# VectorE in place of GpSimd for the whole-tile sums, other first banks in the second FFN layer and its row work issued tile by tile

## The chip, the core and the metric

The kernel runs on one core of one Trainium2 chip. A core has TensorE (PE in the profile; its weight loads are PEld), VectorE (DVE), ScalarE (ACT), GpSimd (POOL) and SyncE (SP), which here only issues DMAs. Each engine works through its own queue in order. The metric is the device time in microseconds.

## The reference

One trunk layer is applied to two groups of rows with the same parameters: 1024 latent rows (the sample) and 128 prompt rows, 1152 rows of width 1024. First comes a mixing sub-layer of four gated branches, which this change does not touch until its last product, the output projection. Then an FFN of hidden width 2816, and a final norm:

```
x  = x + g1 * (merged @ w_o)                 # output projection
h2 = rmsnorm(x, norm2_g) * (1 + sc2) + sh2
a, b = split(h2 @ ffn_w1)                    # 1024 -> 2 x 2816
x  = x + g2 * ((silu(a) * b) @ ffn_w2)       # 2816 -> 1024
y  = rmsnorm(x, final_norm_g)
```

Everything is float32.

## The kernel before

Every float32 operand of a matmul is split in two parts of a rounded format: a high part (ScalarE casts it) and the rest (VectorE subtracts the high part from the source). A product of two operands is then three matmuls into the same bank (mm3, lines 257 to 259; lines 1372 to 1374 in the first FFN layer). So each tile that TensorE reads costs one ScalarE and one VectorE instruction, whatever else it needs.

Both FFN layers use a two-by-two block scheme with seven block products in place of eight (products 0 to 6). It needs sums and differences of blocks of the weights (S1 to S4), of the activations (T1 to T4) and of the results. A sum of 128x512 elements is called a whole-tile sum here.

The stages that matter:

*Output projection* (lines 1450 to 1477). Three column groups c of 384 rows each, two halves hf of 512 columns. For each, TensorE multiplies into three banks; VectorE multiplies them by the gate g1 into xt (line 1472), the sum with x is made by GpSimd for c = 0 and 1 and by VectorE for c = 2 (line 1473), ScalarE sums squares (line 1474), and the new x goes to DRAM (x1_d, line 1476). norm_to_quarters (line 1283) then normalises a group, transposes it on TensorE in four steps kp and makes the sums of its quarters: two on VectorE (lines 1300, 1301), two on GpSimd (1302, 1303), all of 128x192, and splits them (1306, 1307).

*First FFN layer*. Twenty-two pairs j of a gate tile and a value tile, seven products each. w_prepare(j, i) (line 1327) makes the weight tile of product i, three products ahead (LEAD = 3): it loads the raw weights at i = 0, sums blocks with GpSimd at i = 1, 4 and 5 (w_sum, line 1322), casts (1340) and subtracts (1341). A pair uses four PSUM tiles f0, f1, f3 and f4 of two banks each; Pair.evac (line 1377) reads them out after each product, f1 after product 1, f0 after product 2, f3 after product 5 and f4 after product 6 (line 1396). Pair.store (line 1399) writes the pair's result to DRAM and, for every second pair, forms four whole-tile row sums with GpSimd (line 1414).

*Second FFN layer*. Seven products n of 11 steps jj each. A step multiplies four row tiles q, 12 matmuls; in products 0, 4 and 5 a fifth bank, pp, takes three more matmuls for the prompt rows (ask_part, "ask" in the names), whose share of product 6 stands at the end. prepare(n, jj) (line 1549) is called three steps ahead: it takes the next tile from the generator weights(jj) (line 1526), which loads blocks into br (16 buffers) and forms differences with GpSimd (lines 1532, 1536, 1540), loads the row tile ar (4 buffers), and splits both (parts, lines 1522 and 1523) into ah and bh (4 buffers each), or for some tiles into slot, a pool of 10 buffers (line 1258). A pool J of eight banks is opened before the first product (line 1579). After the eleven steps evacuate(n, q) (line 1642) reads out each bank. From product 4 on it also does the row work in the same place: residual (times g2, plus x1), squares, first_half (times the final norm's weight) and finish (norm, output). Of these the sums on lines 1611, 1627 and 1651 and the product on line 1622 are GpSimd's. The power of -1/2 in every norm is GpSimd's as well (line 280).

What sets the order: the program is traced in the order of the Python code, and a scheduler then places each engine's instructions by a simulated time, earlier code first where several are ready; a block under high priority or ahead(n) moves up. Buffers are given out in that same pass. So the code's order is a preference, and the order on an engine is fixed when the kernel is built.

Of the kernel before, what the change touches and what calls it, by code (L numbers as in the profile page):

```python
# [15 lines left out]
P = 128  # L16
# [68 lines left out]
def kernel(ctx: ExitStack, tc: tile.TileContext, A: dict, O: dict):  # L85
# [1197 lines left out]
    def norm_to_quarters(xn3, c):  # L1283

        cs = c * CH
        for kp in range(4):
# [15 lines left out]
            G.tensor_sub(u[1][:, 0], b22, b12)  # L1302
            G.tensor_sub(u[1][:, 1], b21, u[0][:, 1])
# [23 lines left out]
    def w_prepare(j, i):  # L1327
# [3 lines left out]
        if i == 1:  # L1331
            w_sum(j, "S1", "A21", "A22", G.tensor_add)
            w_sum(j, "S2", "S1", "A11", G.tensor_sub)
        if i == 4:
            w_sum(j, "S3", "A11", "A21", G.tensor_sub)
        if i == 5:
            w_sum(j, "S4", "A12", "S2", G.tensor_sub)
# [12 lines left out]
    class Pair:  # L1350
# [48 lines left out]
        def store(self):  # L1399
# [12 lines left out]
            for o, t, x, y, op in (("S1", s1, a21, a22, G.tensor_add), ("S2", s2, s1, a11, G.tensor_sub),  # L1412
                                   ("S3", s3, a11, a21, G.tensor_sub), ("S4", s4, a12, s2, G.tensor_sub)):
                op(t, x, y)
                put(o, t)
# [32 lines left out]
    for c in range(NCH):  # L1448
        sts = [small("wst", [P, 4], bufs=4) for _ in range(3)]
        for hf in range(2):  # L1450
# [18 lines left out]
            for q in range(3):  # L1469
# [3 lines left out]
                (V if c == NCH - 1 else G).tensor_add(x, x, t)  # L1473
# [52 lines left out]
    def weights(jj):  # L1526
# [3 lines left out]
        for kh, nh in ((0, 1), (1, 1)):  # L1530
            x = w2_load(kh, nh, jj)
            G.tensor_sub(x, x, b)
# [3 lines left out]
        G.tensor_sub(x, b21, b)  # L1536
# [3 lines left out]
        G.tensor_sub(x, b22, b12)  # L1540
# [8 lines left out]
    def prepare(n, jj):  # L1549
# [5 lines left out]
        bt = zt("bh", [P, 2, 512], 4, F32R) if n < 6 or jj < 4 else slot("bh", [P, 2, 512], F32R)  # L1555
# [3 lines left out]
        elif n in PROMPT:  # L1559
            plain[n, jj] = ready[n, jj][1]  # L1560

# [17 lines left out]
    open_psum("J", "left", m=8)  # L1579
# [5 lines left out]
    for h in range(2):  # L1585
        hs = slice(h * KH, h * KH + KH)
        dma(askr[:, hs], ask_d[h])
# [16 lines left out]
    def residual(i, h, c):  # L1604
# [6 lines left out]
        G.tensor_add(c, c, x1)  # L1611
# [6 lines left out]
    def first_half(i, c):  # L1618
# [3 lines left out]
        G.tensor_mul(c, c, fng[:, :512])  # L1622

    def last_product(i, c, ps):
        t = half_slot("lp")
        V.tensor_mul(t, ps, g2rows[i == 8][:, 512:])
        G.tensor_add(c, c, t)
# [14 lines left out]
    def evacuate(n, q, ps):  # L1642
# [6 lines left out]
        elif n == 2:  # L1649
            V.tensor_add(a["c21"], a["c11"], ps)  # L1650
            G.tensor_add(a["c12"], a["c12"], a["c21"])
        elif n == 3:
            V.tensor_add(a["c21"], a["c21"], ps)
        elif n == 4:
            V.tensor_add(a["c11"], a["c11"], ps)
            first_half(q, a["c11"])
        elif n == 5:
            V.tensor_add(a["c21"], a["c21"], ps)
            V.tensor_add(a["c22"], a["c12"], ps)
            residual(q, 1, a["c12"])  # L1660
            first_half(4 + q, a["c21"])
            residual(4 + q, 1, a["c22"])
            finish(4 + q, a["c21"], a["c22"])
# [4 lines left out]
    def ask_part(n, pp, jj):  # L1668
        kh, nh = PROMPT[n]
        k = kh * KH + jj  # L1670
        mm3(pp, (askt[:, 0, k], askt[:, 1, k]), plain.pop((n, jj)), jj == 0, jj == KH - 1)
# [15 lines left out]

    def product(n, qs):
        ps = {q: bank("f2", "m") for q in qs}
        pp = bank("fp", "m") if n in PROMPT and n < 6 else None  # L1690
        for jj in range(KH):
# [7 lines left out]
            if pp is not None:  # L1699
                ask_part(n, pp, jj)  # L1700
# [5 lines left out]
    for n in range(7):  # L1706
# [9 lines left out]
        product(n, range(4))  # L1716
    pp = bank("fp", "m")
# [160 lines left out]
```

## Time and profile before

| what | value |
|---|---|
| median of 3 timed runs | 2130.51 us (2131.29, 2124.45, 2130.51) |
| the profiled execution's own time | 2123.89 us |
| its span, first to last instruction | 2122.1 us |
| mean granted clock of TensorE | 0.987 |
| GpSimd busy, instructions | 575.8 us, 516 |

The stages in the span: projection to about 1303 us, then the norm of the last group and the first pair to 1378, the first FFN layer to 1848, the second to 2108, and a tail without matmuls. In the views, a row of a group names its line, engine and operation, then output<-inputs, the shapes, the count, busy us and mean ns of one, and at the end the idle time in front of it with what ended it. "PE f L259 <- DVE ah L1523: 4.9, 2, 4.4" means that TensorE's instructions of line 259 waited 4.9 us in total for VectorE's of line 1523, in two waits, the longest of 4.4. A busy share is an average over a stretch, so each stage is read by itself.

### The profile page before, as it was taken

What the parts mean: (1) busy time and instruction counts of PE and PEld (TensorE: products, weight loads), DVE (VectorE), ACT (ScalarE), POOL (GpSimd) and SP (SyncE); (2) the same over time, 40 slices, a digit from 0 to 9 for tenths busy, and PEclk for the clock granted to TensorE, in tenths of its full rate; (3) what the DMA queues carried; (4) which work ended last, traced back from release to release, by engine and by line L of the source; (5) the groups of instructions that cost most, each with busy time, mean ns of one, the idle gap of its engine ahead of it and who ended that gap; (6) DMA issues with size and microseconds to landing.
All of it is one profiled execution on the core that took longest, in us unless ns stands there. A gap on an engine that the chain in (4) does not pass through costs nothing.

```text
span 2122.1 us, 32144 instructions
## 1 busy us (share of the span) xinstructions
PE 2035.4 (96%) x12268; PEld 1816.2 (86%) x12268; DVE 1293.3 (61%) x2193; ACT 785.9 (37%) x1440; POOL 575.8 (27%) x516
## 2 busy tenths in 40 slices
PE   6899999999999999999999997899999999999996
PEld 1558888898888799999999975799999999978784
DVE  4833499934434268998923257644554545596688
ACT  3734453446431532332223245422222222244353
POOL 1210020000001201222212135244454443383247
PEclk9999999999999999999999998899999999999998
DMA  7684563124233263232131244122232222474543
GB/s 286 203 275 154 191 198 107 63 85 146 84 123 100 94 199 105 90 128 82 61 100 62 84 173 149 65 89 78 88 116 79 104 78 78 178 265 130 202 130 129
DMA packets 140958, 273.37 MB, mean 129 GB/s; under 512 B 16898, under 2 KB 75363, under 8 KB 140676
## 3 DMA queue, kind: packets, MB, share of 16 engines
q1 hardware_dynamic: 131348, 242.61, 34.4%
q0 software_dynamic: 8160, 26.35, 3.2%
q8 instruction: 96, 1.57, 0.3%
q10 hardware_dynamic: 1296, 2.36, 0.3%
q14 instruction: 58, 0.48, 0.1%
HBM read 198.02 MB, written 73.24 MB: 128 GB/s over the span
## 4 chain that ended last, share of the span: by engine, by line
PE 70%; DVE 8%; DMA 3%; issue 3%; ACT 2%; POOL 1%; SPq 0%; POOLq 0%; DVEq 0%; ACTq 0%
PE gm L257 8%; PE gm L259 8%; PE gm L258 8%; PE f L1373 7%; PE f L1374 7%; PE f L1372 7%; PE po L682 2%; PE f L259 2%; PE f L258 2%; PE f L257 2%; PE ptr L672 2%; PE po L258 1%; PE po L259 1%; PE po L257 1%; PE wo L258 1%
## 5 line engine op out<-in xcount | busy, mean ns | idle before, releaser
L257 PE MATMUL gm<-hT_hi,whi 128*128 128x384 f32 x1224 | 420.0, 343 | 1.6 <-ACT sg L1174 1.6
L259 PE MATMUL gm<-hT_hi,wlo 128*128 128x384 f32 x1224 | 418.7, 342 | 2.8 <-DVE wlo L233 2.8
L258 PE MATMUL gm<-hT_lo,whi 128*128 128x384 f32 x1224 | 416.2, 340 | 0.0
L257 PEld LDWEIGHTS gm<-hT_hi,whi 128*128 128x128 f32 x1224 | 230.0, 188 | 12.3 <-issue 7.5
L259 PEld LDWEIGHTS gm<-hT_hi,wlo 128*128 128x128 f32 x1224 | 230.0, 188 | 11.3 <-issue 5.1
L258 PEld LDWEIGHTS gm<-hT_lo,whi 128*128 128x128 f32 x1224 | 230.0, 188 | 5.7 <-issue 3.8
L1372 PE MATMUL f<-xa_hi,wf 128*128 128x288 f32 (+2 forms) x704 | 209.6, 302 | 6.2 <-DVE xt L1472 5.1
L1373 PE MATMUL f<-xa_lo,wf 128*128 128x288 f32 (+2 forms) x704 | 210.7, 300 | 1.9 <-DVE xa_lo L1307 1.9
L1374 PE MATMUL f<-xa_hi,wf 128*128 128x288 f32 (+2 forms) x704 | 208.8, 300 | 1.4 <-DVE wf L1341 1.3
L1179 POOL TENSOR_TENSOR mg<-mg,sg 128x384 f32<-128x384 f32 x72 | 97.6, 1357 | 363.5 <-DVE sg L1175 359.2
L1373 PE MATMUL f<-xb,wf 128*128 128x288 f32 (+2 forms) x528 | 157.2, 298 | 0.9 <-DVE xb L1307 0.9
L1372 PE MATMUL f<-xb,wf 128*128 128x288 f32 (+2 forms) x528 | 157.3, 298 | 0.0
L1374 PE MATMUL f<-xb,wf 128*128 128x288 f32 (+2 forms) x528 | 157.1, 297 | 0.0
L1174 ACT ACTIVATE sg<-gm,vec 128x384 f32<-128x384 f32 x96 | 55.9, 582 | 242.6 <-PE gm L259 237.6
L1372 PEld LDWEIGHTS f<-xa_hi,wf 128*128 128x128 f32 x704 | 133.8, 191 | 7.7 <-ACT wf L1340 6.6
L1373 PEld LDWEIGHTS f<-xa_lo,wf 128*128 128x128 f32 x704 | 135.3, 192 | 2.9 <-DVE xa_lo L1307 2.8
L1374 PEld LDWEIGHTS f<-xa_hi,wf 128*128 128x128 f32 x704 | 134.0, 191 | 2.3 <-DVE wf L1341 2.2
L1175 DVE SCALAR_TENSOR_TENSOR sg<-sg,po 128x384 f32<-128x384 f32 x96 | 52.6, 548 | 125.6 <-PE po L259 119.8
L259 PE MATMUL f<-bh,ah 128*128 128x512 f32 x308 | 120.6, 395 | 4.9 <-DVE ah L1523 4.9
L258 PE MATMUL f<-bh,ah 128*128 128x512 f32 x308 | 121.6, 395 | 1.6 <-DVE bh L1523 1.6
L257 PE MATMUL f<-bh,ah 128*128 128x512 f32 x308 | 119.5, 394 | 2.1 <-DVE st L1396 2.1
L1341 DVE TENSOR_TENSOR wf<-ws,wf 128x512 fp32r<-128x512 f32 x88 | 104.1, 1212 | 2.6 <-ACT wf L1340 2.5
(411 smaller groups left out, 4532.1 us busy)
## 6 DMA issues: line engine op xcount, KB each, us to landing
adaw<-in_ada_w_dram SPq DMA_DIRECT2D x48, 512.0 KB
wraw<-in_w_ffn_dram SPq DMA_DIRECT2D x44, 512.0 KB
wraw<-in_w_gate_dram SPq DMA_DIRECT2D x32, 640.0 KB
br<-in_w_ffn_dram SPq DMA_DIRECT2D x66, 256.0 KB
wraw<-in_w_o_dram SPq DMA_DIRECT2D x24, 512.0 KB
S_d<-rs POOLq DMA_DIRECT2D x44, 256.0 KB, 2.9
ar<-S_d SPq DMA_DIRECT2D x44, 256.0 KB
wraw<-in_w_in_dram SPq DMA_DIRECT2D x19, 512.0 KB
```

Source lines behind the costliest of these rows:

```text
L257: mm(out, ah, bh, start=start, stop=False)
L258: mm(out, ah, bl, start=False, stop=False)
L259: return mm(out, al, bh, start=False, stop=stop)
L672: tr(pt[:, k * P:(k + 1) * P], pe[:, (k0 + k) * P:(k0 + k + 1) * P], ident)
L682: mm(po[64 * j:64 * j + 64, :P], vtile(kt)[:, h * 64:(h + 1) * 64], pT[:, i, :], start=(i == 0), stop=(i == len(kts) - 1))
L1174: S.activation(sg, pg, AF.Tanh, bias=vc("gate_b", b * 8 + j), scale=0.5)
L1175: V.scalar_tensor_tensor(sg, sg, 1.0, po, op0=ALU.add, op1=ALU.mult)
L1179: G.tensor_add(merged[j][:, cs], merged[j][:, cs], sg)
L1341: V.tensor_sub(t[:, 1], src, f(t[:, 0]))
L1372: mm(out, w[:, 0, ks], x[0], start=st, stop=False, skip_group_check=True)
L1373: mm(out, w[:, 0, ks], x[1], start=False, stop=False, skip_group_check=True)
L1374: mm(out, w[:, 1, ks], x[0], start=False, stop=sp_, skip_group_check=True)
```

## The change

Every whole-tile sum, difference or product that GpSimd does from the output projection on, and the two sums of 192 columns in norm_to_quarters, is done by VectorE instead. GpSimd keeps its DMA issues and the power of line 280.

In the second FFN layer: product 0 takes its banks from f0, f1 (row tiles) and f3 (prompt), and pool J is opened after it. The first eight of the eleven prompt blocks are loaded and split before the last pair ends (ask_early), into three slot buffers. The split weights of product 4 go to slot and those of product 5 as before to the four bh buffers. The prompt's matmuls of product 4 lag two steps. The row work that followed products 4 and 5 is put on a list, rest, of which one entry is issued after every second step of the next product.

```
--- before.py
+++ after.py
@@ -1299,8 +1299,8 @@
             b11, b12, b21, b22 = v[:, 0, 0], v[:, 0, 1], v[:, 1, 0], v[:, 1, 1]
             V.tensor_sub(u[0][:, 0], b12, b11)
             V.tensor_sub(u[0][:, 1], b22, u[0][:, 0])
-            G.tensor_sub(u[1][:, 0], b22, b12)
-            G.tensor_sub(u[1][:, 1], b21, u[0][:, 1])
+            V.tensor_sub(u[1][:, 0], b22, b12)
+            V.tensor_sub(u[1][:, 1], b21, u[0][:, 1])
             for (dst, o, n, src) in ((xav, 0, 2, v[:, :, 0]), (xav, 2, 2, u[0]), (xbv, 0, 2, u[1]), (xbv, 2, 1, v[:, 1:2, 1])):
                 hi, lo = dst[0][:, o:o + n, c, kp], dst[1][:, o:o + n, c, kp]
                 S.copy(hi, src)
@@ -1329,12 +1329,12 @@
         if i == 0:
             raw_load(j)
         if i == 1:
-            w_sum(j, "S1", "A21", "A22", G.tensor_add)
-            w_sum(j, "S2", "S1", "A11", G.tensor_sub)
+            w_sum(j, "S1", "A21", "A22", V.tensor_add)
+            w_sum(j, "S2", "S1", "A11", V.tensor_sub)
         if i == 4:
-            w_sum(j, "S3", "A11", "A21", G.tensor_sub)
+            w_sum(j, "S3", "A11", "A21", V.tensor_sub)
         if i == 5:
-            w_sum(j, "S4", "A12", "S2", G.tensor_sub)
+            w_sum(j, "S4", "A12", "S2", V.tensor_sub)
         t = slot("wf", [P, 2, 512], F32R)
         src = raws[j][PRODUCTS[i][0]]
         S.copy(t[:, 0], src)
@@ -1409,8 +1409,8 @@
             put("A12", a12)
             put("A22", a22)
             s1, s2, s3, s4 = (t[:, i] for t in (slot("rs", [P, 2, 512]) for _ in range(2)) for i in range(2))
-            for o, t, x, y, op in (("S1", s1, a21, a22, G.tensor_add), ("S2", s2, s1, a11, G.tensor_sub),
-                                   ("S3", s3, a11, a21, G.tensor_sub), ("S4", s4, a12, s2, G.tensor_sub)):
+            for o, t, x, y, op in (("S1", s1, a21, a22, V.tensor_add), ("S2", s2, s1, a11, V.tensor_sub),
+                                   ("S3", s3, a11, a21, V.tensor_sub), ("S4", s4, a12, s2, V.tensor_sub)):
                 op(t, x, y)
                 put(o, t)
 
@@ -1470,7 +1470,7 @@
                 x = x1s[q][:, hs]
                 t = half_slot("xt")
                 V.tensor_mul(t, b3[q], g1rows[3 * c + q == 8][:, hs])
-                (V if c == NCH - 1 else G).tensor_add(x, x, t)
+                V.tensor_add(x, x, t)
                 S.activation(t, x, AF.Square, accum_out=sts[q][:, hf:hf + 1])
         for q in range(3):
             nc.gpsimd.dma_start(x1_d[3 * c + q], x1s[q])
@@ -1529,15 +1529,15 @@
         yield b, None
         for kh, nh in ((0, 1), (1, 1)):
             x = w2_load(kh, nh, jj)
-            G.tensor_sub(x, x, b)
+            V.tensor_sub(x, x, b)
             b = x
             yield b, None
         b21, x = w2_load(1, 0, jj), zt("br", [P, 512], 16)
-        G.tensor_sub(x, b21, b)
+        V.tensor_sub(x, b21, b)
         yield x, None
         yield b21, None
         b22, b12, x = w2_load(1, 1, jj), w2_load(0, 1, jj), zt("br", [P, 512], 16)
-        G.tensor_sub(x, b22, b12)
+        V.tensor_sub(x, b22, b12)
         yield x, b12
         yield b22, None
 
@@ -1552,12 +1552,23 @@
         at = zt("ah", [P, 2, 512], 4, F32R)
         ar = zt("ar", [P, 512], 4)
         dma(ar, rows_d[SECOND[n], jj])
-        bt = zt("bh", [P, 2, 512], 4, F32R) if n < 6 or jj < 4 else slot("bh", [P, 2, 512], F32R)
+        bt = zt("bh", [P, 2, 512], 4, F32R) if n not in (4, 6) or n == 6 and jj < 4 else slot("bh", [P, 2, 512], F32R)
         ready[n, jj] = parts(at, ar), parts(bt, raw)
         if extra is not None:
             plain[n, jj] = parts(slot("bx", [P, 2, 512], F32R), extra)
         elif n in PROMPT:
             plain[n, jj] = ready[n, jj][1]
+
+    first_ask = {}
+
+    def ask_early():
+
+        raw = slot("askr", [P, 8, P])
+        dma(raw, ask_d[0][:, :8])
+        hi, lo = (slot("ask", [P, 8, P], F32R) for _ in range(2))
+        S.copy(hi, raw)
+        V.tensor_sub(lo, raw, f(hi))
+        first_ask.update({jj: (hi[:, jj], lo[:, jj]) for jj in range(8)})
 
     steps = [(n, jj) for n in range(7) for jj in range(KH)]
     order = [(j, i) for h in range(NF) for j in (h // 2 + h % 2 * KH,) if j for i in range(7)]
@@ -1576,15 +1587,15 @@
             open_z()
             for st_ in steps[:LEAD]:
                 prepare(*st_)
-    open_psum("J", "left", m=8)
+            ask_early()
 
     big = wide["right"].tile([P, 6912], F32, tag="xb0", name="rows2", bufs=1)
     g2rows = [big[:, :D], big[:, D:2 * D]]
     fng, cp, askr = big[:, 2 * D:3 * D], big[:, 3 * D:4 * D], big[:, 4 * D:].rearrange("p (k n) -> p k n", n=P)
     askt = wide["right"].tile([P, 2, NF, P], F32R, tag="xb1", name="ask", bufs=1)
     for h in range(2):
-        hs = slice(h * KH, h * KH + KH)
-        dma(askr[:, hs], ask_d[h])
+        hs = slice(8 - 8 * h if not h else KH, h * KH + KH)
+        dma(askr[:, hs], ask_d[h][:, 0 if h else 8:])
         S.copy(askt[:, 0, hs], askr[:, hs])
         V.tensor_sub(askt[:, 1, hs], askr[:, hs], f(askt[:, 0, hs]))
 
@@ -1608,7 +1619,7 @@
             x1 = half_slot("x1")
             dma(x1, x1_d[i][:, h * 512:h * 512 + 512])
         V.tensor_mul(c, c, g2rows[i == 8][:, h * 512:h * 512 + 512])
-        G.tensor_add(c, c, x1)
+        V.tensor_add(c, c, x1)
 
     def squares(i, h, c):
         if i not in stats:
@@ -1619,12 +1630,12 @@
 
         residual(i, 0, c)
         squares(i, 0, c)
-        G.tensor_mul(c, c, fng[:, :512])
+        V.tensor_mul(c, c, fng[:, :512])
 
     def last_product(i, c, ps):
         t = half_slot("lp")
         V.tensor_mul(t, ps, g2rows[i == 8][:, 512:])
-        G.tensor_add(c, c, t)
+        V.tensor_add(c, c, t)
 
     def finish(i, c0, c1):
 
@@ -1648,19 +1659,22 @@
             S.copy(a["c12"], ps)
         elif n == 2:
             V.tensor_add(a["c21"], a["c11"], ps)
-            G.tensor_add(a["c12"], a["c12"], a["c21"])
+            V.tensor_add(a["c12"], a["c12"], a["c21"])
         elif n == 3:
             V.tensor_add(a["c21"], a["c21"], ps)
         elif n == 4:
             V.tensor_add(a["c11"], a["c11"], ps)
-            first_half(q, a["c11"])
+            rest.append(lambda: first_half(q, a["c11"]))
         elif n == 5:
             V.tensor_add(a["c21"], a["c21"], ps)
             V.tensor_add(a["c22"], a["c12"], ps)
-            residual(q, 1, a["c12"])
-            first_half(4 + q, a["c21"])
-            residual(4 + q, 1, a["c22"])
-            finish(4 + q, a["c21"], a["c22"])
+
+            def done():
+                residual(q, 1, a["c12"])
+                first_half(4 + q, a["c21"])
+                residual(4 + q, 1, a["c22"])
+                finish(4 + q, a["c21"], a["c22"])
+            rest.append(done)
         else:
             last_product(q, a["c12"], ps)
             finish(q, a["c11"], a["c12"])
@@ -1668,7 +1682,7 @@
     def ask_part(n, pp, jj):
         kh, nh = PROMPT[n]
         k = kh * KH + jj
-        mm3(pp, (askt[:, 0, k], askt[:, 1, k]), plain.pop((n, jj)), jj == 0, jj == KH - 1)
+        mm3(pp, first_ask.get(k, (askt[:, 0, k], askt[:, 1, k])), plain.pop((n, jj)), jj == 0, jj == KH - 1)
 
     def ask_evac(n, pp):
         kh, nh = PROMPT[n]
@@ -1685,9 +1699,16 @@
             last_product(8, c, pp)
             finish(8, cp[:, :512], c)
 
+    lagged, rest = [], []
+
     def product(n, qs):
-        ps = {q: bank("f2", "m") for q in qs}
-        pp = bank("fp", "m") if n in PROMPT and n < 6 else None
+        if n == 0:
+            two = [four.tile([P, 2, 512], F32, tag=f"f{i}", name=nm("f2"), bufs=1) for i in (0, 1)]
+            ps = {q: two[q // 2][:, q % 2] for q in qs}
+            pp = four.tile([P, 2, 512], F32, tag="f3", name=nm("fp"), bufs=1)[:, 0]
+        else:
+            ps = {q: bank("f2", "m") for q in qs}
+            pp = bank("fp", "m") if n in PROMPT and n < 6 else None
         for jj in range(KH):
             s = steps.index((n, jj)) + LEAD
             if s < len(steps) and steps[s] not in ready:
@@ -1697,7 +1718,13 @@
                 ts_ = slice(q * P, q * P + P)
                 mm3(ps[q], (ah[:, ts_], al[:, ts_]), b, jj == 0, jj == KH - 1)
             if pp is not None:
-                ask_part(n, pp, jj)
+                lagged.append((n, pp, jj))
+                if len(lagged) > (2 if n == 4 else 0):
+                    ask_part(*lagged.pop(0))
+            if jj % 2 and rest:
+                rest.pop(0)()
+        while lagged:
+            ask_part(*lagged.pop(0))
         for q in qs:
             evacuate(n, q, ps[q])
         if pp is not None:
@@ -1714,6 +1741,10 @@
                 dma(t, x1_d[i])
                 x1s.update({(i, h): t[:, h * 512:h * 512 + 512] for h in range(2)})
         product(n, range(4))
+        if n == 0:
+            open_psum("J", "left", m=8)
+    while rest:
+        rest.pop(0)()
     pp = bank("fp", "m")
     for jj in range(KH):
         ask_part(6, pp, jj)
```

More of the change, by code (lines that the diff above doesn't have):

```diff
@@ L1554, in prepare @@
         dma(ar, rows_d[SECOND[n], jj])
-        bt = zt("bh", [P, 2, 512], 4, F32R) if n < 6 or jj < 4 else slot("bh", [P, 2, 512], F32R)
+        bt = zt("bh", [P, 2, 512], 4, F32R) if n not in (4, 6) or n == 6 and jj < 4 else slot("bh", [P, 2, 512], F32R)
         ready[n, jj] = parts(at, ar), parts(bt, raw)
@@ L1560, in prepare, with ask_early @@
             plain[n, jj] = ready[n, jj][1]
+    first_ask = {}
+    def ask_early():
+        raw = slot("askr", [P, 8, P])
+        dma(raw, ask_d[0][:, :8])
+        hi, lo = (slot("ask", [P, 8, P], F32R) for _ in range(2))
+        S.copy(hi, raw)
+        V.tensor_sub(lo, raw, f(hi))
+        first_ask.update({jj: (hi[:, jj], lo[:, jj]) for jj in range(8)})
     steps = [(n, jj) for n in range(7) for jj in range(KH)]
@@ L1659, in evacuate, with done @@
             V.tensor_add(a["c22"], a["c12"], ps)
[L1660 to L1663, printed above, removed]
+            def done():
+                residual(q, 1, a["c12"])
+                first_half(4 + q, a["c21"])
+                residual(4 + q, 1, a["c22"])
+                finish(4 + q, a["c21"], a["c22"])
+            rest.append(done)
         else:
@@ L1686, in ask_evac @@
             finish(8, cp[:, :512], c)
+    lagged, rest = [], []
     def product(n, qs):
-        ps = {q: bank("f2", "m") for q in qs}
-        pp = bank("fp", "m") if n in PROMPT and n < 6 else None
+        if n == 0:
+            two = [four.tile([P, 2, 512], F32, tag=f"f{i}", name=nm("f2"), bufs=1) for i in (0, 1)]
+            ps = {q: two[q // 2][:, q % 2] for q in qs}
+            pp = four.tile([P, 2, 512], F32, tag="f3", name=nm("fp"), bufs=1)[:, 0]
+        else:
+            ps = {q: bank("f2", "m") for q in qs}
+            pp = bank("fp", "m") if n in PROMPT and n < 6 else None
         for jj in range(KH):
@@ L1699, in product @@
             if pp is not None:
-                ask_part(n, pp, jj)
+                lagged.append((n, pp, jj))
+                if len(lagged) > (2 if n == 4 else 0):
+                    ask_part(*lagged.pop(0))
+            if jj % 2 and rest:
+                rest.pop(0)()
+        while lagged:
+            ask_part(*lagged.pop(0))
         for q in qs:
@@ L1716 @@
         product(n, range(4))
+        if n == 0:
+            open_psum("J", "left", m=8)
+    while rest:
+        rest.pop(0)()
     pp = bank("fp", "m")
```

42 lines of the change are left out of this document (21 added, 21 removed).

## The prediction

> **What bounds the kernel now.** I read the page first, then busy time by stage, then what TensorE waited for.
>
> ```profile
> PE 2035.4 (96%) x12268; PEld 1816.2 (86%) x12268; DVE 1293.3 (61%) x2193; ACT 785.9 (37%) x1440; POOL 575.8 (27%) x516
> ```
>
> TensorE is busy 96% of the span of 2122.1 us. A gain can only come out of the 87 us in which it isn't, or out of stretches at a lower clock. The stages that the change touches, as the view of busy time by window gives them (stretch and its length; busy us and instructions of TensorE, its weight loads, VectorE, ScalarE and GpSimd; granted clock, DMA share, GB/s):
>
> ```profile
> 1262.00:1378.00 116.00, 94.47 (x441) 77.76 (x440) 84.53 (x141) 62.83 (x132) 45.75 (x50) 0.87 0.28 102
> 1378.00:1848.00 470.00, 470.00 (x3527) 470.00 (x3527) 241.62 (x294) 117.61 (x209) 201.08 (x211) 1.00 0.27 93
> 1848.00:1880.00 32.00, 28.36 (x124) 22.45 (x123) 28.54 (x21) 12.76 (x19) 23.85 (x20) 1.00 0.96 360
> 1960.00:1996.00 36.00, 30.89 (x126) 24.35 (x125) 22.75 (x31) 12.83 (x24) 9.35 (x8) 0.95 0.64 220
> 2060.00:2092.00 32.00, 27.12 (x112) 21.27 (x111) 32.00 (x33) 11.97 (x29) 23.18 (x14) 0.95 0.20 58
> 2105.30:2122.10 16.80, 2.54 (x12) 1.73 (x10) 10.29 (x18) 7.22 (x15) 9.36 (x10) 0.73 0.42 157
> ```
>
> TensorE idles 21.5 us from the end of the projection to the first pair (1262 to 1378), nothing in the first FFN layer (470 of 470), and 3.6, 5.1 and 4.9 us at three places of the second; then comes a tail of 14.3. In the second layer, from 1848 on, it waited for:
>
> ```profile
> PE f L259 <- DVE ah L1523: 4.9, 2, 4.4
> PE fp L257 <- DVE c L1653: 3.8, 1, 3.8
> PE f L257 <- DVE st L1396: 2.1, 1, 2.1
> PE f L258 <- DVE bh L1523: 1.6, 3, 0.9
> PE fp L259 <- DVE ask L1589: 1.3, 1, 1.3
> ```
>
> VectorE is named each time. Is it slow by itself, or held up? The groups answer, first those of the first FFN layer, then those of the second:
>
> ```profile
> L1341 DVE TENSOR_TENSOR wf<-ws,wf 128x512 fp32r<-128x512 f32 x81 | 98.8, 1250 | 0.0
> L1341 DVE TENSOR_TENSOR wf<-wraw,wf 128x512 fp32r<-128x512 f32 x61 | 41.6, 682 | 0.0
> ```
>
> ```profile
> L1322 POOL TENSOR_TENSOR ws<-wraw 128x512 f32<-128x512 f32 x20 | 25.7, 1286 | 26.1 <-DMA wraw<-in_w_ffn_dram 25.9
> ```
>
> ```profile
> L1523 DVE TENSOR_TENSOR ah<-ar,ah 128x512 fp32r<-128x512 f32 x75 | 79.6, 1064 | 30.6 <-ACT ah L1522 28.0 <-DMA br<-in_w_ffn_dram 2.3
> L1523 DVE TENSOR_TENSOR bh<-br,bh 128x512 fp32r<-128x512 f32 x74 | 71.7, 977 | 0.1
> L1610 DVE TENSOR_TENSOR c<-c,rows 128x512 f32<-128x512 f32 x16 | 21.6, 1378 | 0.0
> ```
>
> One and the same subtraction on line 1341 takes 682 ns, or 1250 where its source is a fresh GpSimd sum and GpSimd is adding beside it. In the second layer, where GpSimd prepares the weights all along, none of VectorE's splits keeps the 682: 1064, 977, 1378. GpSimd's work costs VectorE time that VectorE's own rows are charged with.
>
> **Part by part.** *Price of a moved sum.* Line 1473 runs on both engines already, so the view of that line prices the move (shortest, median and longest in ns; GpSimd's are stretched too); beside it stand narrower VectorE groups of the same stage:
>
> ```profile
> L1473 POOL TENSOR_TENSOR x<-x,xt x6: 1281/1308/2273, 1277.7 to 1288.1; 128x512 f32<-128x512 f32 x6
> L1473 DVE TENSOR_TENSOR x<-x,xt x6: 675/680/686, 1317.9 to 1343.3; 128x512 f32<-128x512 f32 x6
> ```
>
> ```profile
> L1307 DVE TENSOR_TENSOR xa_lo<-nv,xa_hi 128x384 fp32r<-128x384 f32 x11 | 8.7, 792 | 0.3 <-ACT xa_hi L1306 0.2
> L1307 DVE TENSOR_TENSOR xb<-nv,xb 128x192 fp32r<-128x192 f32 x12 | 8.2, 679 | 0.0
> L1472 DVE TENSOR_TENSOR xt<-wo,g1r 128x512 f32<-128x512 f32 x12 | 7.9, 678 | 1.7 <-PE wo L259 1.7
> L1307 DVE TENSOR_TENSOR xb<-nu,xb 128x384 fp32r<-128x384 f32 x12 | 7.2, 601 | 0.0
> L1307 DVE TENSOR_TENSOR xa_lo<-nu,xa_hi 128x384 fp32r<-128x384 f32 x12 | 6.5, 545 | 0.0
> ```
>
> A whole tile costs 0.68 us on VectorE; the line through 678 ns at 512 columns and 545 at 384 gives 0.35 for 192, an estimate.
>
> *Projection and first pair.* Moved: 24 sums of 192 columns (8.4 us), 6 of line 1473 (4.1) and 8 of line 1322 (5.4), 17.9 in all. Returned by two rows alone: 11 x (792-545) ns and 12 x (679-345) ns, 6.7 us. So VectorE gets up to 11.2 us more in a stage of 116 in which it is busy 84.5 and TensorE waits for it; on the other hand each quarter of the norm loses two hops between engines. Ends: -6.7 (only what is returned counts) and +11.2 (all the rest lies on the path). I take 0, as the two effects pull against each other on the same queue.
>
> *First FFN layer.* Moved: 80 weight sums and 40 row sums, 120 x 0.68 = 81.6 us; returned 81 x (1250-682) ns = 46. VectorE goes from 241.6 to 277 of 470, and TensorE waits for nothing here: 0. The cover is VectorE's remaining 193 us. What it costs if that cover goes is the fourth case below: the first weight sum waits for its load (25.9 us in 20 pairs), and behind it on VectorE stand the evacuations that free PSUM.
>
> *Start of the second layer.* Its first banks are now taken from tiles f0, f1 and f3, which are read out before the pair's last product (only f4 waits for it); the wait for line 1396 (2.1 us) goes. The first eight prompt blocks come in before the last pair ends, so the 1.3 us for line 1589 goes too: their 0.5 MB on SP's queue pass ahead of later weight loads but leave a window with a DMA share of 0.96, and their cast and subtraction fall into the covered stage. New is that the eight banks of pool J open after the first product: the second product's first bank waits for a ScalarE copy, under the three row tiles that follow (2.1 us at 0.23 us a matmul, nine of them). Sum -3.4; ends -3.6 and 0, the latter if a wait of 2.1 moves to the second product and the loads set the rest.
>
> *Third to fifth product.* The 3.8 us wait is for a bank that the prompt's product needs; its matmuls now lag two steps behind (two times twelve matmuls at 0.23, 5.5 us), so TensorE has other work in that time. After the wait it also ran slowly:
>
> ```profile
> 1984.37 0.39 PE L259 MATMUL f<-bh,ah 128*128 128x512 f32 x1
> 1984.60 0.39 PE L257 MATMUL f<-bh,ah 128*128 128x512 f32 x1
> ...
> 1991.31 0.63 PE L257 MATMUL f<-bh,ah 128*128 128x512 f32 x1
> 1991.73 0.63 PE L258 MATMUL f<-bh,ah 128*128 128x512 f32 x1
> ```
>
> From start to start 0.42 in place of 0.23 us, over eight matmuls: 1.5 us more. The Trainium skill ("TensorE: Matmul & The Clock Gate", Part 1) says that the clock halves after about 3.4 us of idling; the trace agrees (3.8 us, then half speed), and by that rule a wait shortened below this would already win the 1.5. Wait and slow matmuls are 5.3. Weight tiles of the fifth product take other buffers (slot), so those of the next can't run ahead as far; the waits for bh (1.6) stay. I take -4.5; ends -6.6 and 0.
>
> *Last product.* The residual work of products five and six, until now one batch at their ends, is issued at every second step of the following product. VectorE was busy 32 of 32 us when TensorE waited the 4.4 and 0.5 us for ah, and lost 16 x (1378-680) ns = 11 us in line 1610 over the layer. After: a batch for one row tile is seven whole tiles (4.8) and about 1.1 of small ones and scaling, four of them 23.6; evacuation of eight banks 5.4, prompt 1.4, eight steps of splitting 10.9: 41 us, beside eleven steps of fifteen matmuls at 0.23, 38 us. It is nearly full, but with nothing blocked, and the splits no longer stand behind the whole batch. Loads of x1 now pass between those of ar on SP's queue, which has four buffers of ar to live on. The wait of 4.4 exceeds the 3.8 after which the matmuls ran slowly, so about 1.5 hangs on it as well (an estimate). I take -4 of these 6.4; ends -6.4 and +3, the excess of 41 over 38.
>
> *Tail.* From the chain that ended last:
>
> ```profile
> 2103.25 0.70 DVE lp L1626
> ...
> 2106.61 0.17 DVE fst L1634
> 2106.78 0.07 issue
> 2106.85 0.56 POOL fst L280
> 2107.41 0.02 issue
> 2107.43 0.75 DVE c L1639
> 2108.18 1.15 DVE fst L1633
> ...
> 2117.31 0.75 DVE rows L1639
> ```
>
> In this chain VectorE's 128x1 addition takes 1.15 us, behind GpSimd's sum. It lasts from 2103.25 to 2118.06, 14.8. After, with two small ones of 0.17, five times (0.68 + 0.68 + 0.34 + 0.75) = 12.2 on one engine: -2.6, rounded to -3 as the first of them can start under the last matmuls; ends -4 (line 1633 at 0.17 in place of 1.15, four times) and 0. The power on line 280 stays on GpSimd (0.56). The Trainium skill ("SBUF — State Buffer", Who interferes with whom) says that a two-input VectorE instruction is blocked for the whole of a GpSimd one that reads SBUF; by it five powers would give back up to 2.8 of this gain. Line 1341's rows agree with it in kind.
>
> Sum: 0 + 0 - 3.4 - 4.5 - 4 - 3 = -14.9, on the profiled execution's 2123.9: 2109.0. That execution is 6.6 below the median of the three timed runs (2130.5) and 3.6 below the mean of all four (2127.5); I add 3.6: 2112.5. About 0.3%, 6.4 us, can be told from no change.
>
> **Rivals.** *VectorE becomes the bound of the last two products.* For: 41 us of work against 38, and the order is the scheduler's, not mine. Against: it had the same work, blocked, and TensorE lost only 4.9. The last product then gains nothing and the one before loses 4: 2120.5.
> *The waits only move.* The loads and their buffers, not VectorE, pace the products: at 1848 to 1880 the DMA share is 0.96, and VectorE sat 28.0 us waiting for ScalarE's casts of ah. Then 1.3 of the start and the tail's 3 remain: 2123.2.
> *Slower: VectorE's queue stands at the weight sums.* In the first FFN layer it waits for each load, as GpSimd did (25.9 us); that decides the time where the load comes later than the two or three products for which the banks last. All of it on the path, the rest as forecast: 2123.9 - 14.9 + 25.9 + 3.6 = 2138.5. Against: TensorE has not one wait there, and VectorE is free for half of the time.
>
> **How the numbers follow.** Forecast 0.52, VectorE bound 0.22, waits move 0.17, slower 0.09. Range 2100 to 2126: it leaves out the fourth case and the ends of the first and third, about 0.17. Faster than 2124.1: the first case, 0.16 of the second, 0.08 of the third, 0.76; slower: 0.06 of the fourth; the rest 0.18.
>
> **What would show it.** Line 1341 and lines 1523 and 1610 at one length of 680 ns; GpSimd with little but line 280 and DMA issues; no TensorE wait for lines 1396, 1589 and 1653; that for ah under 1 us; clock 1.00 around 1990; tail under 13 us; first FFN layer still 470 of 470. A TensorE wait over 4 us for VectorE in the projection or in the last product, or any in the first FFN layer, would make it wrong.

## The result

The changed kernel takes 2096.18 us (median of 5 runs, 2093.11 to 2097.43), the kernel before 2124.7 in the 5 runs beside it (2123.29 to 2131.29). The ratio is 0.9854, 95% interval 0.9834 to 0.9873, or 1.46% faster; the medians lie 28.5 us apart. 2112.5 was forecast and 2100 given as the lower end. The sign was right, and so was the main mechanism, a VectorE held up by GpSimd; the stages were forecast to win 14.9 us, about half of what they won.

The profiled execution took 2097.43 us, with a span of 2095.3 in place of 2122.1. The page's row of the engines, after:

```profile
PE 2028.1 (97%) x12268; PEld 1814.3 (87%) x12268; DVE 1295.1 (62%) x2442; ACT 785.4 (37%) x1441; POOL 243.5 (12%) x268
```

VectorE has 249 instructions more, 248 of them GpSimd's and one for the early prompt blocks, and is busy for only 1.8 us more (1295.1 against 1293.3). So GpSimd's 332 us of sums had cost VectorE about as much as VectorE now spends on doing them. TensorE's idle time fell from 86.7 us (2122.1 - 2035.4) to 67.2, and its busy time by 7.3, since it runs fewer matmuls at the lower clock (mean granted clock 0.990 in place of 0.987). 19.5 and 7.3 make the 26.8 us of the span.

Busy time by window (stretch and length; busy us and instructions of TensorE, its weight loads, VectorE, ScalarE, GpSimd; clock, DMA share, GB/s), after:

```profile
1262.00:1371.00 109.00, 92.05 (x440) 77.57 (x439) 82.78 (x172) 60.02 (x127) 8.65 (x14) 0.89 0.32 114
1371.00:1837.00 466.00, 466.00 (x3501) 466.00 (x3500) 263.82 (x407) 116.09 (x206) 48.59 (x90) 1.00 0.26 91
1837.00:1870.00 33.00, 33.00 (x158) 27.80 (x157) 25.31 (x39) 14.93 (x24) 3.78 (x7) 1.00 1.00 380
1870.00:1960.00 90.00, 90.00 (x399) 74.53 (x398) 67.59 (x110) 45.62 (x82) 0.00 (x0) 1.00 0.56 180
1960.00:2060.00 100.00, 100.00 (x436) 81.45 (x435) 74.25 (x120) 43.62 (x83) 0.00 (x0) 1.00 0.47 151
2060.00:2080.50 20.50, 20.50 (x90) 16.52 (x89) 17.00 (x35) 8.74 (x19) 4.57 (x4) 1.00 0.43 151
2080.50:2095.30 14.80, 1.45 (x7) 0.83 (x5) 8.81 (x23) 6.54 (x15) 2.74 (x5) 0.67 0.48 178
```

From 1371 to the end of the second layer TensorE is busy all the time at full clock. Before, it idled 13.6 us between 1848 and 2105. In the two windows from 1870 to 2060 VectorE is busy for three quarters of the time. From 1262 up to its last matmul, all of TensorE's waiting lies ahead of 1371.

The groups of VectorE, first of the first FFN layer, then of the second (line 1621 is line 1610 of before):

```profile
L1341 DVE TENSOR_TENSOR wf<-ws,wf 128x512 fp32r<-128x512 f32 x80 | 53.0, 683 | 0.0
```

```profile
L1523 DVE TENSOR_TENSOR ah<-ar,ah 128x512 fp32r<-128x512 f32 x75 | 51.4, 685 | 23.7 <-ACT ah L1522 23.4
L1523 DVE TENSOR_TENSOR bh<-br,bh 128x512 fp32r<-128x512 f32 x74 | 50.0, 684 | 1.8 <-ACT bh L1522 1.8
...
L1621 DVE TENSOR_TENSOR c<-c,rows 128x512 f32<-128x512 f32 x16 | 10.6, 680 | 0.0
```

The means of 1250, 1064, 977 and 1378 ns have all become 680 to 685. The 149 splits of the second layer take 101.4 us in place of 151.3.

The four means of before mix short instructions with long ones, which the view of a line (shortest, median and longest in ns) shows in the kernel before:

```profile
L1341 DVE TENSOR_TENSOR wf<-ws,wf x81: 681/683/5280, 1377.5 to 1829.4; 128x512 fp32r<-128x512 f32 x81
L1610 DVE TENSOR_TENSOR c<-c,rows x16: 677/1762/1787, 2024.4 to 2086.8; 128x512 f32<-128x512 f32 x16
```

Most instructions either kept their 0.68 us or were held for one or several of GpSimd's sums. On line 1341, of the 80 that start in the first FFN layer, 70 took 0.68 us and ten took 5.28; of the 74 splits into bh in the second layer 54 took 0.68 and 20 took 1.7 to 1.8.

From here on I compare stages, each measured in a kernel's profiled execution between the same matmuls: the first and the last of the output projection; the last of the first FFN layer; the last for sample rows in the second; the end of the span. What lies ahead of the projection is in none of them. The projection's last matmuls stand at 1321 to 1341 in the kernel before, among the first of the next layer, so its stage reaches beyond the 1303 that I gave above. us:

| kernel | projection | to the end of the first FFN layer | second FFN layer | rest | sum |
|---|---|---|---|---|---|
| before | 134.6 | 506.9 | 256.9 | 17.2 | 915.6 |
| after | 127.4 | 506.9 | 239.2 | 15.1 | 888.6 |
| after, a second time | 127.1 | 504.9 | 239.7 | 15.2 | 886.9 |

The gain is 7.2 us in the projection, 17.7 in the second layer and 2.1 behind it. Two profiles of the same kernel differ by up to 2 us in a stage, so smaller differences say nothing here.

### The profile page after: what moved, and what is told of

It is laid out like the page before. It is cut to its first block, busy times and chain, and to the rows that moved or that the text cites. A ratio compares the mean times of both kernels' runs of the same rounds, so it can differ in the third digit from the quotient of the medians.

```text
span 2095.3 us, 31997 instructions
## 1 busy us (share of the span) xinstructions
PE 2028.1 (97%) x12268; PEld 1814.3 (87%) x12268; DVE 1295.1 (62%) x2442; ACT 785.4 (37%) x1441; POOL 243.5 (12%) x268
## 4 chain that ended last, share of the span: by engine, by line
PE 83%; DVE 6%; issue 4%; DMA 4%; ACT 1%; SPq 1%; POOL 1%; POOLq 0%; DVEq 0%; ACTq 0%
PE gm L257 9%; PE gm L259 9%; PE gm L258 9%; PE f L1372 8%; PE f L1374 8%; PE f L1373 8%; PE f L259 3%; PE f L257 3%; PE f L258 3%; PE po L682 3%; PE ptr L672 2%; PE po L258 1%; PE po L259 1%; PE sp L345 1%; PE po L257 1%
## 5 line engine op out<-in xcount | busy, mean ns | idle before, releaser
L1174 ACT ACTIVATE sg<-gm,vec 128x384 f32<-128x384 f32 x96 | 55.9, 582 | 243.2 <-PE gm L259 242.9
L1374 PEld LDWEIGHTS f<-xa_hi,wf 128*128 128x128 f32 x704 | 134.6, 191 | 0.1
L258 PE MATMUL f<-bh,ah 128*128 128x512 f32 x308 | 120.3, 391 | 0.0
L257 PE MATMUL f<-bh,ah 128*128 128x512 f32 x308 | 119.1, 390 | 0.0
L259 PE MATMUL f<-bh,ah 128*128 128x512 f32 x308 | 118.1, 391 | 0.0
L1340 ACT CAST wf<-ws 128x512 fp32r<-128x512 f32 x88 | 51.2, 615 | 154.2 <-DVE ws L1322 153.2
```

The source lines that it names most:

```text
L257: mm(out, ah, bh, start=start, stop=False)
L258: mm(out, ah, bl, start=False, stop=False)
L259: return mm(out, al, bh, start=False, stop=stop)
L1174: S.activation(sg, pg, AF.Tanh, bias=vc("gate_b", b * 8 + j), scale=0.5)
L1340: S.copy(t[:, 0], src)
L1374: mm(out, w[:, 1, ks], x[0], start=False, stop=sp_, skip_group_check=True)
```

## The experiments

The theory: GpSimd's sums hold up VectorE's instructions beside them, and TensorE loses time wherever it waits for VectorE; the gain comes from taking these sums off GpSimd and hardly from the new order (A). The rivals: the order won the time, by the lag, the row work by steps and the first banks (B); GpSimd's results simply came late, and VectorE's are ready sooner (C); VectorE is now nearly the bound and has eaten a part of the gain (D).

**The sums alone.** The kernel before, with every G of the diff as V and nothing else, for example

```
-            G.tensor_sub(x, x, b)
+            V.tensor_sub(x, x, b)
```

> The kernel before with every moved sum on VectorE, and nothing else changed. Theory A (GpSimd's reads held VectorE up, and that was behind most of the waits): the 7.3 us before the first FFN layer and the 2 us of the tail come back whole, and at least two thirds of the 17.5 us of the second layer, as VectorE's splits fall to 685 ns: about 2103 to 2106. Theory B (the second layer's waits came from its banks and from the order of the row work, and only went with those edits): only the first two come back, and TensorE still waits for lines 1396, 1589, 1653 and 1523 there: about 2115.

2101.42 us (2098.22 to 2106.72, 4 runs), ratio 0.9890 (0.9868 to 0.9913). Projection and first FFN layer took 635.5 us together (641.5 before, 634.3 after), the second layer 245.7, the rest 15.0; the sum is 896.2, 19.4 below before. The time lies a little below the 2103 to 2106 of A. TensorE's waits in the second layer, of this kernel (total us, times, longest):

```profile
PE f L257 <- DVE st L1396: 2.9, 1, 2.9
PE fp L257 <- DVE c L1653: 0.3, 1, 0.3
```

The waits for ah, bh and ask are gone without any reordering, and the 3.8 us for c of line 1653, to which I had given a lag of two steps, is down to 0.3. Only that for the first bank stays.

**The order alone.** The changed kernel with all those sums on GpSimd again, for example

```
-            V.tensor_sub(x, x, b)
+            G.tensor_sub(x, x, b)
```

> The kernel after with every moved sum back on GpSimd: only the first banks, the early prompt blocks, the lag, the buffers and the row work by steps are left. Theory A: VectorE's splits stay at about 1000 ns in the second layer and waits for them stay or move; at most 6 us are won there, nothing before: 2118 to 2122. Theory B: the second layer is free of waits or nearly so, 14 to 17 us won, nothing before it: 2108 to 2111.

2120.36 us (2115.0 to 2123.9, 10 runs), ratio 0.9972 (0.9960 to 0.9984). The second layer took 251.9, the sum of the stages 911.1, 4.5 below before. In the second layer TensorE waited for:

```profile
PE f L259 <- DVE ah L1523: 8.1, 1, 8.1
PE f L258 <- DVE bh L1523: 1.3, 4, 0.5
```

The first bank's wait and that for the prompt's bank are gone, so these edits do what they say; but one wait for ah of 8.1 us stands where there were two of 4.9 in all. The chain of this kernel up to it (start, us, what):

```profile
2067.29 1.97 DVE c L1621 x2
2069.26 0.25 issue
2069.51 5.08 DVE c L1621 x3
2074.59 1.68 DVE ah L1523
```

Three products by g2 took 5.08 us in place of three times 0.68, and the split that TensorE waited for 1.68. Issued step by step or not, the row work is slow while GpSimd adds beside it. 19.4 and 4.5 make 23.9 of the 27.0 us. That the 3.1 left over come only with both isn't shown: by the ratios 0.9890 times 0.9972 is 0.9862, inside the interval of the changed kernel.

**The row work in one batch.** The changed kernel with

```
-            rest.append(lambda: first_half(q, a["c11"]))
+            first_half(q, a["c11"])
...
-            rest.append(done)
+            done()
```

> The kernel after, but the row work of products 4 and 5 stands again in one batch at their ends. Theory A: an unblocked VectorE gets through the batch (about 24 us of work) within the four steps that are prepared ahead, or nearly so: at most 2 us, 2096 to 2098. Theory B: the wait for ah in the last product comes back with its slow matmuls, 5 to 7 us: 2101 to 2103.

2096.45 us (2094.76 to 2097.6, 4 runs), ratio 0.9863 (0.9848 to 0.9877); second layer 240.6, and not one wait of TensorE in it. The row work by steps earns nothing.

**The old first banks.** The changed kernel with pool J opened ahead of product 0 and without ask_early:

```
-            ask_early()
+    open_psum("J", "left", m=8)
```

> The kernel after, but the second layer opens its eight banks before its first product and loads the prompt blocks after the first layer, as before. The bank wait for line 1396 (2.1 us) does not depend on GpSimd and should come back under both theories: 2098 to 2099. The wait for the prompt's split on line 1589 (1.3 us) comes back under theory B (2099 to 2100) and not under A, since VectorE stood behind GpSimd's sums there.

2102.7 us (2098.28 to 2103.96, 4 runs), ratio 0.9889 (0.9873 to 0.9905); second layer 242.9, with one wait:

```profile
PE f L257 <- DVE st L1396: 2.4, 1, 2.4
```

First banks and early prompt blocks had 3.4 us in the forecast; by the stage they are worth 3.7 (242.9 against 239.2), of which 2.4 is the wait. The wait for the prompt's ask (1.3 us before) does not come back without ask_early. 2098 to 2100 was expected. By the medians the edit costs 6.5 us, and the ranges don't overlap; but the first matmul of the projection, ahead of which it changes nothing, stands at 1209.3 us in this kernel's profile and at 1206.8 in the changed one's, which is 2.5 of it. The last run below, which has these edits but none of the lag, buffers and steps, gives 5.5 for them against the sums alone (240.2 and 245.7).

**Sums on both engines.** The changed kernel in which GpSimd, beside nearly every moved sum (not for lines 1473, 1633 and 1662), adds its two sources, or one of them to itself, and writes the result into a scratch tile that nobody reads:

```
+    def again(x, y):
+        G.tensor_add(ghost[:, :x.shape[-1]], x, y)
...
             V.tensor_sub(x, x, b)
+            again(b, b)
```

> The kernel after, in which GpSimd also adds the source tiles of nearly all moved sums into a scratch tile that nobody reads (not those of lines 1473, 1633 and 1662). VectorE and the order of the program stay. Theory A (while GpSimd reads, VectorE's two-input instructions stand): VectorE's splits in the second layer go back to 900 to 1060 ns, and at least half of the gain is lost: 2108 to 2120. Theory C (GpSimd's sums were only late, 1.3 to 1.8 us and two hops between engines in a chain): VectorE stays at 685 ns, TensorE waits for nothing new, 2096 to 2099.

2154.65 us (2151.26 to 2157.77, 4 runs), ratio 1.0129 (1.0112 to 1.0145): 58 us slower than the changed kernel, and far above the 2108 to 2120 of A. The projection took 132.8 us, the second layer 271.4, the rest 26.1. Two groups of this kernel's second layer and its first wait there (its lines stand 9 later):

```profile
L1532 DVE TENSOR_TENSOR ah<-ar,ah 128x512 fp32r<-128x512 f32 x76 | 73.9, 975 | 13.8 <-ACT ah L1531 13.7
L1532 DVE TENSOR_TENSOR bh<-br,bh 128x512 fp32r<-128x512 f32 x76 | 65.7, 872 | 0.8 <-ACT bh L1531 0.8
```

```profile
PE f L258 <- DVE bh L1532: 18.8, 15, 2.3
```

VectorE still makes every result itself, and yet its splits are back at means of 975 and 872 ns from 685, and TensorE waits for those of bh fifteen times. That speaks for A and against C. One thing runs along with it: GpSimd reads the source tiles, so they come free later and some loads start later. A load that starts later doesn't lengthen a subtraction, so the lengths are shown; how the 58 us divide isn't, nor whether a part of the 27.0 us came by C as well.

**The sums twice on VectorE.** The changed kernel with the moved sums of lines 1532, 1536, 1540, 1622 and 1638 each joined by one more addition of that size on VectorE, 67 in all, into the same scratch tile:

```
+    def again(x, y):
+        V.tensor_add(ghost[:, :x.shape[-1]], x, y)
```

> The kernel after, with each moved sum of the second FFN layer (80 less the products of line 1633 and the sums of line 1662) done twice on VectorE, the second time into a scratch tile. It tells how much room VectorE has there: 67 instructions of 0.68 us, 46 us more. If it is nearly the bound of the last two products, as the second case of the prediction had it, 8 us or more are lost: 2104 and up, with TensorE waits for lines 1523. If there is room, what is lost lies in the tail alone, five times 0.6: 2098 to 2100.

2105.22 us (2103.34 to 2111.78, 4 runs), ratio 0.9902 (0.9882 to 0.9922). Busy time of this kernel by window, the second layer and what comes behind its last matmul for sample rows:

```profile
1834.20:2079.00 244.80, 244.80 (x1082) 201.15 (x1080) 212.82 (x353) 111.80 (x204) 6.10 (x10) 1.00 0.57 189
2079.00:2101.40 22.40, 0.16 (x1) 0.00 (x0) 17.30 (x38) 7.51 (x16) 4.78 (x6) 0.58 0.38 141
```

VectorE is now busy 212.8 of 244.8 us (184 in the four windows of the changed kernel), and TensorE still never waits; the rest grew from 15.1 to 22.6, by more than the five times 0.6 that I expected with room. VectorE's order of time there has eleven of the additions: the five of line 1638 and six of line 1622, which it had not come to before the last matmul. So D is wrong for the products, which took 29 us of sums more (212.8 - 184) without a wait of TensorE, and right for the tail, where every VectorE instruction counts.

**The first FFN layer on GpSimd.** The changed kernel with lines 1322 and 1414 as before, of which the first is

```
-            w_sum(j, "S1", "A21", "A22", V.tensor_add)
+            w_sum(j, "S1", "A21", "A22", G.tensor_add)
```

> The kernel after with the sums of the first FFN layer (lines 1322 and 1414) back on GpSimd, those of the first pairs among them. Theory A with the cover of the prediction: in the layer itself line 1341 goes back to about 1250 ns on fresh sums and TensorE still waits for nothing; only the first pairs' eight sums, beside the norm, cost up to 3 us: 2096 to 2099. Rival: the moved sums of that layer carry a part of the gain, since later loads and the end of the layer hang on them: 2100 or more.

2093.85 us (2091.26 to 2096.58, 4 runs), ratio 0.9843 (0.9825 to 0.9861), a little below the 2096 to 2099 of A. Line 1341 in this kernel's first FFN layer, and the layer's window:

```profile
L1341 DVE TENSOR_TENSOR wf<-ws,wf 128x512 fp32r<-128x512 f32 x80 | 98.3, 1260 | 0.0
```

```profile
1370.00:1836.00 466.00, 466.00 (x3497) 465.83 (x3496) 240.09 (x288) 117.46 (x208) 201.05 (x210) 1.00 0.26 92
```

VectorE is held as it was before, and TensorE works 466 of 466 us. The largest part of the change, 132 of its 248 sums (120 of them inside this layer), is worth nothing here, either way.

**Without lag and with the old buffers.** The changed kernel with

```
-                if len(lagged) > (2 if n == 4 else 0):
+                if len(lagged) > 0:
```

and with bh for the split weights of product 4.

> The kernel after, with the prompt's matmuls of product 4 not lagging and its split weights in the four bh buffers as before. Theory A: the wait of 3.8 us for line 1653 was VectorE's, which stood behind a split; with VectorE unblocked it does not come back: within 1.5 us of the kernel after, 2095 to 2098. Theory B (the lag removed it, as the prediction had it): 3.8 us and 1.5 us of slow matmuls come back, 2100 to 2102.

2096.72 us (2092.53 to 2097.72, 4 runs), ratio 0.9853 (0.9838 to 0.9869); second layer 238.2, no wait in it. Neither earns anything.

**The projection on GpSimd.** The changed kernel with lines 1302, 1303 and 1473 as before, 36 sums:

```
-            V.tensor_sub(u[1][:, 0], b22, b12)
+            G.tensor_sub(u[1][:, 0], b22, b12)
...
-                V.tensor_add(x, x, t)
+                (V if c == NCH - 1 else G).tensor_add(x, x, t)
```

> The changed kernel with only the sums of the output projection and of its norm (lines 1302, 1303 and 1473) on GpSimd as before. If the held VectorE cost the projection its time, projection and first FFN layer together go back from 634 to about 641 us, with waits of TensorE for ntr and for the splits of line 1306 and 1307, and the kernel takes 2102 to 2104. If the 7 us there came from the first FFN layer's sums or from the spread between executions, it stays at 2096.

2103.34 us (2101.97 to 2105.03, 4 runs), ratio 0.9902 (0.9887 to 0.9917). Beside it on the same chip the changed kernel itself:

> The changed kernel itself once more, beside the other two on one chip: 2096 within 3 us, 634 us for projection and first FFN layer together, 239 for the second layer to its last sample matmul, 15 behind it.

2095.57 us (2094.86 to 2098.66, 4 runs), ratio 0.9868 (0.9853 to 0.9883). The projection takes 133.8 us with GpSimd's sums and 127.1 without. One of VectorE's groups from 1255 on in the kernel with GpSimd's sums, and then in the changed one:

```profile
L1128 DVE TENSOR_TENSOR wlo<-wraw,whi 128x1024 fp32r<-128x1024 f32 x12 | 15.5, 1292 | 3.2 <-ACT whi L1127 3.2
```

```profile
L1128 DVE TENSOR_TENSOR wlo<-wraw,whi 128x1024 fp32r<-128x1024 f32 x12 | 14.7, 1222 | 2.9 <-ACT whi L1127 2.6
```

The waits of the projection's own matmuls (wo), with GpSimd's sums and then in the changed kernel:

```profile
PE wo L258 <- DVE wlo L1128: 2.8, 3, 1.6
PE wo L257 <- DVE xt L1472: 1.7, 1, 1.7
PE wo L257 <- ACT whi L1127: 0.2, 1, 0.2
```

```profile
PE wo L257 <- ACT whi L1127: 1.4, 2, 1.0
PE wo L258 <- DVE wlo L1128: 0.9, 3, 0.4
```

The thirty-six sums on GpSimd are worth 6.7 us of the stage and 7.8 of the median. They hold the split of the projection's own weights (line 1128), and the read-out that frees the next bank (line 1472) comes late. As a wait for ScalarE's casts (whi) grows, these rows make 2.4 us of the 6.7 (4.7 against 2.3). The norm's transposes wait 1.4 less (for nv, 3.1 against 1.7), and fewer matmuls run at the lower clock (granted 0.95 and 0.97 in the stage); the rest isn't divided.

**What is left with an effect.** The edits of three runs together in the changed kernel: the first FFN layer's sums on GpSimd, no lag and the old buffers, the row work in a batch. What stays are the sums of the projection and the second layer on VectorE, the first banks and ask_early.

> The changed kernel cut down to what earlier runs left with an effect: the sums of the first FFN layer (lines 1322 and 1414) on GpSimd again, no lag of the prompt matmuls, the old buffers for the split weights of products 4 and 5, the row work issued in batches; the other moved sums on VectorE, the other first banks and the early prompt blocks kept. If the parts put back earn nothing and do not lean on each other, it is as fast as the changed kernel, 2096 within 4 us, without a wait of TensorE in the second layer. If they cover for each other (without the lag the row work by steps hides the wait, without the steps the lag does), waits for c, ah or bh return in the second layer and it takes 2102 to 2106.

2094.19 us (2092.4 to 2096.77, 4 runs), ratio 0.9856 (0.9839 to 0.9872): as fast as the changed kernel (2095.57) and not measurably faster. The second layer takes 240.2 us, and one wait of 0.3 us is left in it.

## Why the prediction was half right

**Held VectorE: right in kind, with a mean misread.** The lengths of lines 1341, 1523 and 1610 went to 680 to 685 as forecast, and unread sums lengthened the splits again. But I took 1250 ns for the length that line 1341 has where its source is a fresh sum of GpSimd's. It is the mean of many at 0.68 us and ten at 5.28, and what those ten stood beside are the row sums of line 1414, not the weight sums (last section). Nor is it so that none of the second layer's splits kept the 682 ns: most did.

By the letter of my last sign there is even a wait that makes this wrong:

```profile
PE f L1372 <- DVE xt L1472: 5.0, 1, 5.0
```

It stands at the first pair's start, for the read-out of a projection bank. The kernel before has it too, with 5.1 us; I hadn't listed it, so the sign could not tell the cases apart, and the change leaves it as it is.

**The sum of the terms: wrong in its size.** The forecast lay 16.3 us above the median. By term:

| term | forecast | by the stages |
|---|---|---|
| projection and first pair | 0 (-6.7 to +11.2) | -7.2 |
| first FFN layer | 0 | 0 |
| second FFN layer, three terms | -11.9 (ends -16.6) | -17.7 |
| tail | -3 | -2.1 |
| from the profiled execution to the median | +3.6 | -1.2 |

The rows differ by 16.9 us in sum; the 0.6 beyond 16.3 lie ahead of the projection and outside of the span.

The step that failed first is "I take 0, as the two effects pull against each other on the same queue". I priced VectorE's load there, 17.9 us to be added and 6.7 returned, and the load weighed nothing: from 1262 to the first pair VectorE's busy time went from 84.5 to 82.8, with 31 more instructions. I had also begun at 1262, though the projection begins at 1206.7; with that part twelve sums of line 1473 move and not six, and from there on VectorE's busy time went from 111.4 to 113.9 with 47 more instructions. So the return was larger than the two rows that I counted. Line 1128, the split of the projection's own weights, was held as well; from 1255 on in the kernel before it is

```profile
L1128 DVE TENSOR_TENSOR wlo<-wraw,whi 128x1024 fp32r<-128x1024 f32 x12 | 16.9, 1406 | 5.3 <-ACT whi L1127 5.3
```

against 1222 ns after. I had begun my groups at the norm and had not looked at it.

The second step is the taking of middles: -4.5 of 6.6, -4 of 6.4, 0 of 6.7. One cause, the held VectorE, stood behind these three, so they came in together: the projection at -7.2, beyond its good end, and the second layer at -17.7 where the good ends of its three terms add up to -16.6. The tail came in at -2.1 of its 4. That all five good ends give -6.7 - 3.6 - 6.6 - 6.4 - 4 = -27.3, where -27.0 was measured, is in part luck, since the tail fell short by about what the others went beyond. My range had these ends in it: 2123.9 - 27.3 + 3.6 is 2100.2, its lower end. What put the measured time below that is the shift of 3.6 (last point of this section): with the -1.2 that was measured in its place, that end is 2095.4.

**What I credited in the second layer: wrong.** I gave the 3.8 us wait and the slow matmuls behind it to the lag, and the 4.4 us to the row work by steps. The sums alone take both waits away; without lag, and without steps, none returns; with steps but on GpSimd, 8.1 us are lost in one place. Only the term of the first banks was credited rightly (-2.1 and a part more; 3.7 measured).

**The cover of the first FFN layer: right**, by the run that puts it back. The fourth case, VectorE's queue standing at the weight sums, did not come: 466 of 466.

**VectorE as the bound of the last two products: wrong.** I had counted 41 us of work beside 38. The last product of the changed kernel by window:

```profile
2045.00:2080.20 35.20, 35.20 (x154) 28.57 (x154) 31.69 (x60) 13.91 (x30) 4.57 (x4) 1.00 0.34 112
```

VectorE is busy 31.7 of 35.2 us. One reason for the 41 shows in its order of time there:

```profile
2043.40 0.68 DVE L1669 TENSOR_TENSOR c<-c,f 128x512 f32<-128x512 f32 x1
2044.00 0.68 DVE L1670 TENSOR_TENSOR c<-c,f 128x512 f32<-128x512 f32 x1
```

Each lasts 0.68 us, but they start 0.60 apart: in a row, a whole tile costs 0.60, and my price of a moved sum was 13% too high.

**The tail: right in kind, a little short.** The chain of the changed kernel at the same place (lp is line 1637 now):

```profile
2078.49 0.70 DVE lp L1637
...
2080.70 0.16 DVE fst L1644
...
2081.54 0.07 issue
2081.61 0.56 POOL fst L280
2082.16 0.02 issue
2082.19 0.75 DVE c L1650
...
2090.30 0.75 DVE rows L1650
```

From 2078.49 to 2091.05 it is 12.6 us in place of 14.8. The addition of 1.15 us is 0.16. I had worked out 12.2, which is near by luck: I left out GpSimd's power (0.56 us and 0.09 around it), which in every round still stands between two VectorE instructions, and put in a second whole tile, lp, which in four of the five rounds runs beside the power or before and costs the chain nothing. One round of the chain takes 0.60 + 0.15 + 0.65 + 0.75 = 2.15. Of the 2.8 us that I had set against the gain, nothing shows: line 1638, with two inputs, keeps 0.69 us. The power on VectorE was not tried.

**The shift of 3.6: wrong.** Two of the three timed runs lay 6.6 and 7.4 us above the profiled execution, and so I added it. Over five runs the median of before is 2124.7, 0.8 above that execution, and the changed kernel's is 1.2 below its own.

## What to carry to other kernels

Where an engine that TensorE waits for is slower on some rows than on others of the same shape, look for GpSimd at work beside it, and price the move of GpSimd's work by the time that is given back in those stretches, not by the load that is added. Such work matters only where TensorE waits (36 sums in the projection were worth 7 us, 132 in the first FFN layer nothing), so choose the sums by stage. Look at shortest, median and longest before pricing by a mean: the mean of line 1341 was no length that any of its instructions in that layer had. Terms with one cause come in together: add their ends, and take the middle once, if at all.

## What was new about the hardware

A two-input VectorE instruction can stand over several GpSimd instructions in a row, not one. In the kernel before, VectorE's and then GpSimd's order of time in the first FFN layer (start, us):

```profile
1581.33 6.48 DVE L1341 TENSOR_TENSOR wf<-ws,wf 128x512 fp32r<-128x512 f32 x3
```

```profile
1582.91 1.30 POOL L1414 TENSOR_TENSOR rs<-hid,hid 128x512 f32<-128x512 f32 x1
1584.15 1.28 POOL L1414 TENSOR_TENSOR rs<-hid 128x512 f32<-128x512 f32 x1
1585.38 0.56 POOL L1406 DMA_DIRECT2D S_d<-rs  x1
1585.95 1.29 POOL L1414 TENSOR_TENSOR rs<-rs,hid 128x512 f32<-128x512 f32 x1
```

Three subtractions took 6.48 us, the longest of them 5.28, while GpSimd made three sums and a DMA issue between them; it ended only after the third. The same length, 5.28 us, stands in the layer ten times, once for each group of row sums. The Trainium skill ("SBUF — State Buffer", Who interferes with whom) says that a VectorE instruction with two inputs contends with a GpSimd one that reads SBUF, and that whoever issues first has the shared ports for its whole instruction. The trace agrees that they contend; read so, a split would lose at most one sum, 1.3 us. The 5.28 shows that it can lose to three in a row, and by its record it even started 0.38 us before the first of them (1582.53 against 1582.91).

The other kind is a taking of turns. In the run with the order alone, GpSimd's order of time beside the three products that took 5.08 us is

```profile
2069.06 3.32 POOL L1622 TENSOR_TENSOR c<-c,x 128x512 f32<-128x512 f32 x2 [0.62 <-DVE c L1621]
2072.34 1.71 POOL L1633 TENSOR_TENSOR c<-c,rows 128x512 f32<-128x512 f32 x1
```

Here each VectorE instruction takes 1.75 us in place of 0.68 and each of GpSimd's 1.7 in place of 1.3, as when each waits for about one of the other's. So the 8.1 us wait of that run came of instructions held for one sum each, many in a row. The ten of 5.28 us cost nothing, as TensorE waits for nothing in that layer. What decides between the two kinds isn't shown.
